# Token operands' remainders one step later on VectorE, and two output accumulators in the statistics' PSUM banks, at the end of layer 1

## The chip, the cores and the metric

The kernel runs on one core of a Trainium2 chip. The metric is the device time of one execution in microseconds (us). Five engines work side by side, each through its own queue in order: TensorE (PE, matrix products into PSUM), VectorE (DVE), ScalarE (ACT), GpSimd (POOL) and SyncE (SP, which issues the DMAs here). They wait for each other through semaphores.

## The reference, cut to what matters

Two layers over 1024 latent tokens of width 1024. Layer 0 mixes by a Fourier transform and differential attention. Layer 1, whose end is the place of the change, is a short gated convolution (`n` is 1024, all in float32):

```python
def short_conv_mixer(proj, conv_w, w_out):
    bg, cg, xt, g = jnp.split(proj, 4, axis=-1)
    u = cg * xt
    ...
    conv = sum(conv_w[t] * up[:, t:t + n] for t in range(CONV_K))
    return (bg * conv * jax.nn.silu(g)) @ w_out
...
    y = short_conv_mixer(h @ odd_w_in[o_i], odd_conv_w[o_i], odd_w_out[o_i])
    ...
    x_lat = x_lat + gate[:, None, :] * y
```

## The kernel before

**Products.** Layer 1 does its two big products (`h @ odd_w_in`, then `y @ odd_w_out`) by a Strassen-like scheme. An output group `g` covers 2 blocks of 128 output features and both halves (512 each) of the tokens. It takes seven products `p` = 1 to 7, written (g, p). Groups 0 to 15 are the input projection, groups 16 to 19 the output projection, 18 and 19 last. Each product combines a weight operand `wop` with four token operands `B[p][k]`, k = 0 to 3. Every operand is split in two, the rounded value and its remainder, so that a product is 4 x 3 matmuls of 128x512 (lines 649 to 651: value by value, value by token remainder, weight remainder by value).

**Accumulators.** The sums of a group stand in three PSUM accumulators: X (products 1, 6, 7, 4 in this order, read out after each), Z (product 2) and Y (products 5, 7 and 3). The pool `acc` has 3 buffers for X, 2 for Y and 1 for Z. The pool `pst`, tag `t`, has 2 more banks; they hold small statistics and transposes earlier in the kernel and nothing at this place. The read-outs of the last four groups are `take` in `finish2` (line 1349, on VectorE): accumulator times gate plus a residual that a DMA has fetched.

**Operands.** `wop` makes a weight operand from raw weights: a rounding copy on ScalarE (line 61), then the remainder on VectorE, or on GpSimd for p = 4 and 7 (line 62). Products 2 and 5 also take additions on GpSimd (line 628). The raw weights of group g + 2 are fetched (`wload`, line 1240) when those of group g are used up. A weight operand is made LEAD = 5 products ahead. `bop` makes a token operand: where the product needs one, a subtraction of two parts of the gated tokens `y` on VectorE (line 1217), then the rounding copy on ScalarE, then the remainder on VectorE, both through `part`.

**Order.** From product (14, 1) on, the order on TensorE, VectorE, ScalarE and GpSimd is that of the code. `order` lists the products:

```python
order += [(16, 1), (16, 5), (17, 1), (17, 5), (16, 2), (16, 6), (17, 2), (17, 6), (16, 7), (17, 7), (16, 4), (16, 3),
          (17, 4), (17, 3)]
```

Before it come (14, 7), (15, 7), (14, 4), (14, 3), (15, 4), (15, 3), behind it the seven of 18 and of 19. `hooks` says behind which product which token operands of the output projection are made: p = 1, 5, 6, 2, 7, 4, 3 between (15, 5) and (17, 1). SP's order is set by a scheduler when the kernel is built.

Of the kernel before, what the change touches and what calls it, by code (L numbers as in the profile page):

```python
# [8 lines left out]
F32 = mybir.dt.float32  # L9
F32R = mybir.dt.float32r  # L10
AF = mybir.ActivationFunctionType
ALU = mybir.AluOpType
# [5 lines left out]
P = 128  # L18
# [11 lines left out]
NB = 512  # L30
# [7 lines left out]
def block_kernel(tc, A):  # L38
    nc = tc.nc
# [3 lines left out]
    def opn(name, side="left", space=None):  # L43
        kw = dict(name=name, bufs=1, side=side, reuse_waits="tile")
        if space is not None:
            kw["space"] = space
        cm = tc.tile_pool(**kw)
        pools[name] = (cm, cm.__enter__())
        return pools[name][1]
# [5 lines left out]
    f32 = lambda t: t.bitcast(F32)  # L55
# [3 lines left out]
    def part(src, o, eng):  # L59

        nc.scalar.copy(out=o[:, 0, :], in_=src)  # L61
        eng.tensor_tensor(out=o[:, 1, :], in0=src, in1=f32(o[:, 0, :]), op=ALU.subtract)  # L62
        return o
# [5 lines left out]
    pst = opn("pst", space=PSUM)  # L69
    acc = opn("acc", space=PSUM)  # L70
# [17 lines left out]
    def load_x(half):  # L88
# [9 lines left out]
        out=cs[:, :, 0:2], in_=small[:, S_C:S_C + 16].rearrange("p (k r) -> p k r", r=2), func=AF.Silu)  # L98
# [5 lines left out]
        out=bias1, in0=small[:, S_B:S_B + 48].rearrange("p (l k) -> p l k", l=2)[:, :, 8:16],  # L104
# [100 lines left out]
    def token_sums(parts, n):  # L205
        ps = pst.tile([P, 8], F32, name="ps_ss", tag="t", bufs=2)
        for i in range(n // P):
            for a in parts:
                nc.tensor.matmul(ps[:, i:i + 1], lhsT=a[:, i * P:(i + 1) * P], rhs=ones[:, 0:1],
                                 start=a is parts[0], stop=a is parts[-1])  # L210
        return ps
# [13 lines left out]
    def ps_rows(dg, n):  # L225

        psr = pst.tile([P, NB], F32, name="ps_r", tag="t", bufs=2)
        nc.tensor.matmul(psr[:, :n], lhsT=ones, rhs=dg[:, :n], start=True, stop=True)
        return psr
# [65 lines left out]
    def proj_tok(tt, c, at=()):  # L295
        ps = acc.tile([P, NB], F32, name="ps_tok", tag="acc", bufs=6)
        for k in range(KT):
            if k in at:
                tick()
            if k == 7:  # L300
                tick(cols)
            proj_step(ps, tt, c, k)
        return ps
# [70 lines left out]
    for k in range(KT):  # L374
        t = hcp.tile([P, TC], F32, name="xc", tag="hc", bufs=17)
# [6 lines left out]
    V, G = nc.vector, nc.gpsimd  # L382
# [66 lines left out]
    ps = token_sums([a0], NB)  # L449
# [148 lines left out]
    for tt in range(NK):  # L598
# [3 lines left out]
        if tt == 0:  # L602
            alds.append(ada_load(*adas[0]))
        ps = proj_tok(tt, 1, (4,))
# [4 lines left out]
                          in_=v.rearrange("p (h d) -> p h d", h=NH))  # L609
# [34 lines left out]
    def quarters(ps, w, x, start, mid=None):  # L644
        for k in range(4):
            if mid and k == mid[0]:
                mid[1]()
            a, b = (w[:, i, k * P:(k + 1) * P] for i in range(2))
            nc.tensor.matmul(ps, lhsT=a, rhs=x[k][0], start=start and k == 0, stop=False, skip_group_check=not start)  # L649
            nc.tensor.matmul(ps, lhsT=a, rhs=x[k][1], start=False, stop=False, skip_group_check=not start)  # L650
            nc.tensor.matmul(ps, lhsT=b, rhs=x[k][0], start=False, stop=k == 3, skip_group_check=not start)  # L651
# [252 lines left out]
    for n, (g, p) in enumerate(order):  # L904
        if ahead:
            q = ahead.pop(0)
# [25 lines left out]
    def w0next(eng=nc.gpsimd):  # L932
        if wq:
            w0half(0, eng)
            w0half(1, eng)
# [139 lines left out]
    def y0(half):  # L1075
        for k in range(KT):
            Y[half][k] = (Yh[half][k], Yl[half][k])

    def proj_feat2(w, half, at={}):
        ps = acc.tile([P, NB], F32, name="ps_feat", tag="acc", bufs=6)  # L1080
        for k in range(KT):
            if k in at:
                at[k]()
            a, b = (w[k // 4][:, i, (k % 4) * P:(k % 4 + 1) * P] for i in range(2))
            nc.tensor.matmul(ps, lhsT=a, rhs=Y[half][k][0], start=k == 0, stop=False)  # L1085
            nc.tensor.matmul(ps, lhsT=a, rhs=Y[half][k][1], start=False, stop=False)  # L1086
            nc.tensor.matmul(ps, lhsT=b, rhs=Y[half][k][0], start=False, stop=k == KT - 1)  # L1087
        return ps
# [63 lines left out]
    acc = opn("acc", space=PSUM)  # L1152
    Y = [[None] * KT for _ in range(2)]
# [36 lines left out]
    def stats1(half):  # L1190
        return rms_diag(token_sums(ssq[half], NB), NB, mp, ("xr", 2))
# [16 lines left out]
        fo_split(*fo, g, nc.gpsimd)  # L1208
    BSRC = {1: 0, 2: 2, 3: 3, 4: 2, 5: 0, 6: 0, 7: 1}

    def bop(p, x, k, eng=None, tt=True):

        q = [*x[k], *x[k + 4 if p not in (1, 5) else k]]
        if tt:
            i = {5: (0, 1, 0), 7: (1, 1, 3), 6: (0, 3, 0), 4: (2, 2, 0)}.get(p)
            if i:
                nc.vector.tensor_tensor(out=q[i[0]], in0=q[i[1]], in1=q[i[2]], op=ALU.subtract)
        o = arena[p - 1][:, k * T:(k + 1) * T].rearrange("p (i t) -> p i t", i=2) if p < 3 else \
            hB.tile([P, 2, NB], F32R, name=f"B{p}", bufs=4)
        B[p][k] = part(q[BSRC[p]], o, eng or nc.vector)  # L1220

    B = {i: [None] * 4 for i in range(1, 8)}

# [7 lines left out]
    def wload(g):  # L1231
        if g < NGR:
            raws[g] = []
            for i in range(2):
                pool = (wp, w2)[g % 2]
                t = pool.tile([P, KT * P], F32, name="wraw", bufs=2)
                if g < 16:
                    nc.sync.dma_start(out=t, in_=A["wodd"][g // 2, ((1, 2), (3, 0))[g % 2][i]])
                else:
                    nc.sync.dma_start(out=t, in_=A["wo1"][2 * (g - 16) + i])  # L1240
                raws[g].append(t)

    def wop(g, p, eng=None):
        pool = wpools[0]
        wpools.append(wpools.pop(0))
        wops[g, p] = wpart(g, p, raws[g], done, lambda: w2.tile([P, NB], F32, name="s1", bufs=1),
                           lambda src, e: part(src, pool.tile([P, 2, NB], F32R, name="wop", bufs=4 if pool is wp else 2), e),
                           eng)
        if p == 3:
            wload(g + 2)  # L1250

    banks = {}

    def product(g, p, mid=None, later=False):
        bank = "ZXZYXYXX"[p]
        start = p in (1, 5, 2)
        if start:
            banks[g, bank] = acc.tile([P, NB], F32, name="ps" + bank, bufs={"X": 3, "Y": 2, "Z": 1}[bank])
        quarters(banks[g, bank], wops.pop((g, p)), [(x[:, 0, :], x[:, 1, :]) for x in B[p]], start, mid)
        fin = finish1 if g < 16 else finish2  # L1260
        if later:
            return lambda: fin(g, p)
        fin(g, p)

    part22 = {}
    us, ysd = {}, []
# [112 lines left out]
    for half in range(2):  # L1379
        y0(half)  # L1380
        for f in range(KT):
            if half == 0 or f < KT - 1:
                w0next()
            if half == 1 and f == KT - 2:
                wload(0)
                wload(1)
            if pend:
                ps = pend.pop(0)
            else:
                ps = proj_feat2(W[half * KT + f], half)  # L1390
            if half == 1 and f == KT - 1:
                for q in order[:5]:
                    wop(*q)
                man.__exit__(None, None, None)
                man = tc.manual_schedule(engines=MANUAL)
                man.__enter__()
            out0(half, f, ps)
            if half == 1 and f == 0:
                dg = stats1(0)
            if half == 1 and f == 1:  # L1400
                r = vv[:, NB:T]
                nc.scalar.copy(out=r, in_=ps_rows(dg, NB))
                mod1(0, range(KT), r)
                for k in range(4):
                    bop(1, x1, k)
                for k in range(4):
                    bop(2, x1, k)

    cls("acc", "pp", "yao")
    acc = opn("wacc", space=PSUM)  # L1410
# [11 lines left out]
    V, G = nc.vector, nc.gpsimd  # L1422
# [77 lines left out]
    for n, (g, p) in enumerate(order):  # L1500
        if n < 12:
            continue
        if (g, p) == (14, 1):
            man.__exit__(None, None, None)
            man = tc.manual_schedule(engines=MANUAL)
            man.__enter__()
        while wn < min(n + LEAD + 1, len(order)):
            wop(*order[wn])
            wn += 1
        product(g, p)  # L1510
        for q, k0, k1 in hooks.get((g, p), ()):
            for k in range(k0, k1):
                bop(q, ysd, k, V)
    man.__exit__(None, None, None)
    cls("hB", "w2", "x1", "m", "w", "wacc", "pst", "at0", "const")

# [100 lines left out]
```

## Time and profile before

| what | value |
|---|---|
| median of 3 runs | 1139.51 us |
| the three runs | 1139.52, 1132.86, 1139.51 us |
| profiled execution, its own time | 1135.15 us |
| its span | 1133.4 us |
| PE busy | 1043.9 us (92% of the span) |
| DVE busy | 763.0 us (67%) |
| mean granted TensorE clock | 0.974 |

The profiled execution is a fourth one beside the three runs. Its span is what the profile covers; 1.75 us of its own time lie around it. Times in views count from the span's start. A timeline row gives the start, the duration, the engine, the line, the operation, what it writes and reads, and in brackets how long the engine was idle before it and who ended that.

### The profile page before, as it was taken

The numbers are of one execution on the slowest core, as the hardware profiler recorded it, in microseconds if no ns is written. First come the engines' busy times: TensorE is split into PE (matmuls) and PEld (weight loads), VectorE is DVE, ScalarE is ACT, GpSimd is POOL, SyncE is SP. The second block draws the span as 40 slices with busy tenths as digits, with TensorE's granted clock in tenths as the row PEclk, the third lists the DMA queues.
The fourth block names the chain that finished last, engine by engine and source line by source line (L and its number), as shares of the span: only waits on it lengthen the run. The fifth ranks groups of instructions, "written<-read, shape, count | busy, mean of one in ns | idle before, by whom it ended". The sixth has DMA issues, their size and how long they took to land.

```text
span 1133.4 us, 14135 instructions
## 1 busy us (share of the span) xinstructions
PE 1043.9 (92%) x5118; PEld 851.1 (75%) x5118; DVE 763.0 (67%) x1073; ACT 480.0 (42%) x868; POOL 498.8 (44%) x422
## 2 busy tenths in 40 slices
PE   4989899989888989999999998889999999998598
PEld 2657688778777878999988876568888888776486
DVE  4599856874868178888873287985645554578642
ACT  4453123311443367777763363633333333343320
POOL 1257103631556236676575455654343444332331
PEclk9999899989899999999999999989999999999799
DMA  9724895434020795271004541121111111111421
GB/s 346 295 94 131 267 296 182 145 112 159 9 93 26 181 262 133 79 182 47 21 20 165 198 165 50 37 75 38 67 46 56 56 57 56 56 67 55 166 76 65
DMA packets 61381, 131.12 MB, mean 116 GB/s; under 512 B 5248, under 2 KB 30208, under 8 KB 58112
## 3 DMA queue, kind: packets, MB, share of 16 engines
q1 hardware_dynamic: 60240, 125.64, 34.8%
q0 software_dynamic: 1072, 4.59, 1.1%
q8 instruction: 40, 0.66, 0.2%
q14 instruction: 29, 0.24, 0.1%
HBM read 105.57 MB, written 24.64 MB: 115 GB/s over the span
## 4 chain that ended last, share of the span: by engine, by line
PE 54%; DVE 16%; POOL 3%; ACT 3%; issue 3%; DMA 3%; SPq 0%; ACTq 0%; DVEq 0%; POOLq 0%
PE psX L649 6%; PE psX L650 6%; PE psX L651 6%; PE ps_av L1032 5%; PE psY L649 3%; PE psY L650 3%; PE psY L651 3%; PE S L982 3%; PE S L983 2%; PE ps_t L1022 2%; DVE nm L987 2%; PE ps_feat L1085 2%; PE ps_feat L1087 2%; PE ps_feat L1086 2%; DVE arena L62 2%
## 5 line engine op out<-in xcount | busy, mean ns | idle before, releaser
L61 ACT CAST wop<-wraw 128x512 fp32r<-128x512 f32 x152 | 93.3, 620 | 130.6 <-PE psY L651 28.0
L62 POOL TENSOR_TENSOR wop<-wraw,wop 128x512 fp32r<-128x512 f32 x72 | 99.7, 1388 | 76.8 <-ACT wop L61 76.4
L284 PE MATMUL ps_tok<-whi,hhi 128*128 128x512 f32 x288 | 119.0, 413 | 3.4 <-ACT hhi L393 2.5
L285 PE MATMUL ps_tok<-whi,hlo 128*128 128x512 f32 x288 | 115.7, 402 | 4.3 <-DVE hlo L397 4.2
L286 PE MATMUL ps_tok<-wlo,hhi 128*128 128x512 f32 x288 | 114.8, 399 | 0.0
L987 DVE TENSOR_REDUCE nm<-S 128x1 f32<-128x1280 f32 x64 | 95.0, 1487 | 22.1 <-PE S L983 20.0
L649 PE MATMUL psX<-B,wop 128*128 128x512 f32 x240 | 97.3, 405 | 9.8 <-ACT c L1293 4.9
L998 ACT ACTIVATE p<-S,nm 128x1280 f32<-128x1280 f32 x64 | 85.2, 1332 | 44.6 <-DVE nm L987 38.9
L650 PE MATMUL psX<-B,wop 128*128 128x512 f32 x240 | 96.9, 404 | 1.5 <-POOL B L1439 1.1
L651 PE MATMUL psX<-B,wop 128*128 128x512 f32 x240 | 96.4, 402 | 0.5 <-POOL wop L62 0.5
L628 POOL TENSOR_TENSOR s<-wraw 128x512 f32<-128x512 f32 x20 | 27.3, 1363 | 120.0 <-DMA wraw<-in_wodd_dram 114.0
L62 DVE TENSOR_TENSOR wop<-wraw,wop 128x512 fp32r<-128x512 f32 x80 | 68.9, 863 | 13.2 <-ACT wop L61 12.9
L628 POOL TENSOR_TENSOR wraw<-wraw 128x512 f32<-128x512 f32 x40 | 56.6, 1421 | 47.9 <-DVE wop L62 40.4
L1032 PE MATMUL ps_av<-v,aT 128*128 128x128 f32 x640 | 76.8, 275 | 0.0
L1032 PEld LDWEIGHTS ps_av<-v,aT 128*128 128x128 f32 x640 | 74.2, 192 | 0.2
L285 PEld LDWEIGHTS ps_tok<-whi,hlo 128*128 128x128 f32 x288 | 55.5, 193 | 18.8 <-DVE hlo L397 8.0
L1009 POOL TENSOR_TENSOR p<-p,cc 128x256 f32<-128x256 f32 x32 | 40.4, 1262 | 65.6 <-DVE cc L1006 46.6
L284 PEld LDWEIGHTS ps_tok<-whi,hhi 128*128 128x128 f32 x288 | 55.7, 193 | 17.8 <-ACT hhi L393 3.7
L649 PE MATMUL psY<-B,wop 128*128 128x512 f32 x160 | 64.1, 400 | 3.6 <-DVE u L1301 1.8
L650 PE MATMUL psY<-B,wop 128*128 128x512 f32 x160 | 64.2, 401 | 0.6 <-POOL B L1439 0.3
L286 PEld LDWEIGHTS ps_tok<-wlo,hhi 128*128 128x128 f32 x288 | 55.4, 192 | 11.9
L651 PE MATMUL psY<-B,wop 128*128 128x512 f32 x160 | 63.7, 398 | 0.0
(344 smaller groups left out, 2671.7 us busy)
## 6 DMA issues: line engine op xcount, KB each, us to landing
ada_raw<-in_ada_dram SPq DMA_DIRECT2D x24, 1024.0 KB, 6.6
wraw<-in_wodd_dram SPq DMA_DIRECT2D x32, 512.0 KB, 3.5
wraw<-in_wo_dram SPq DMA_DIRECT2D x24, 512.0 KB, 3.8
wraw<-in_wtok_dram SPq DMA_DIRECT2D x16, 512.0 KB, 4.2
arena<-kd SPq DMA_DIRECT2D x16, 320.0 KB, 8.6
kq<-kd SPq DMA_DIRECT2D x16, 320.0 KB, 9.7
xt<-in_xT_dram SPq DMA_DIRECT2D x16, 256.0 KB, 5.8
xr<-in_xT_dram SPq DMA_DIRECT2D x16, 256.0 KB, 3.8
```

Source lines behind the costliest of these rows:

```text
L61: nc.scalar.copy(out=o[:, 0, :], in_=src)
L62: eng.tensor_tensor(out=o[:, 1, :], in0=src, in1=f32(o[:, 0, :]), op=ALU.subtract)
L284: nc.tensor.matmul(ps, lhsT=hh, rhs=whi, start=k == 0, stop=False)
L285: nc.tensor.matmul(ps, lhsT=hl, rhs=whi, start=False, stop=False)
L286: nc.tensor.matmul(ps, lhsT=hh, rhs=wlo, start=False, stop=k == KT - 1)
L628: tt = lambda out, x, y, op: nc.gpsimd.tensor_tensor(out=out, in0=x, in1=y, op=op)
L649: nc.tensor.matmul(ps, lhsT=a, rhs=x[k][0], start=start and k == 0, stop=False, skip_group_check=not start)
L650: nc.tensor.matmul(ps, lhsT=a, rhs=x[k][1], start=False, stop=False, skip_group_check=not start)
L651: nc.tensor.matmul(ps, lhsT=b, rhs=x[k][0], start=False, stop=k == 3, skip_group_check=not start)
L987: nc.vector.tensor_reduce(out=nm, in_=S[m][:, :NKEY], op=ALU.max, axis=AX.X, negate=True)
L998: nc.scalar.activation(out=p, in_=S[m][:, :NKEY], func=AF.Exp, bias=tiles.pop((i, m, "nm")), accum_out=z)
L1032: nc.tensor.matmul(ps, lhsT=groups[i, k // 4][:, (k % 4) * P:(k % 4 + 1) * P], rhs=v[:, k * P:(k + 1) * P], start=k == 0, stop=k == NK - 1)
```

## The change

Three things in the code. `bop` no longer calls `part`: the rounding copy is issued on ScalarE as before, and the remainder is put on a list, `lows`. The list is emptied on VectorE by the next `bop`, behind that one's own subtraction (ahead of it where the next `bop` works on the same k, since the subtraction overwrites what the remainder reads), and before a product that needs an operand whose remainder is still on the list. And the accumulators of (16, 5), which is group 16's Y, and of (17, 2), which is group 17's Z, are taken from `pst`, tag `t`, and no more from `acc`.

```diff
-    def bop(p, x, k, eng=None, tt=True):
+    lows = []
+
+    def low():
+
+        for o, src, k in lows:
+            nc.vector.tensor_tensor(out=o[:, 1, :], in0=src, in1=f32(o[:, 0, :]), op=ALU.subtract)
+        lows.clear()
+
+    def bop(p, x, k):
...
+        i = {5: (0, 1, 0), 7: (1, 1, 3), 6: (0, 3, 0), 4: (2, 2, 0)}.get(p)
+        if lows and lows[0][2] == k:
+            low()
+        if i:
+            nc.vector.tensor_tensor(out=q[i[0]], in0=q[i[1]], in1=q[i[2]], op=ALU.subtract)
+        low()
...
-        B[p][k] = part(q[BSRC[p]], o, eng or nc.vector)
+        nc.scalar.copy(out=o[:, 0, :], in_=q[BSRC[p]])
+        lows.append((o, q[BSRC[p]], k))
+        B[p][k] = o
...
-            banks[g, bank] = acc.tile([P, NB], F32, name="ps" + bank, bufs={"X": 3, "Y": 2, "Z": 1}[bank])
+            banks[g, bank] = pst.tile([P, NB], F32, name="ps" + bank, tag="t", bufs=2) if (g, p) in ((16, 5), (17, 2)) \
+                else acc.tile([P, NB], F32, name="ps" + bank, bufs={"X": 3, "Y": 2, "Z": 1}[bank])
...
+        if any(B[p][k] is l[0] for l in lows for k in range(4)):
+            low()
         product(g, p)
```

Line numbers behind the edit move: the token subtraction of line 1217 stands in 1227 afterwards, the token remainder of line 62 in 1216, the read-out of line 1349 in 1363.

**VectorE, at the token operands of p = 5 and 6.** Before, around the products (15, 6) and (15, 2); `B_8194` to `B_8261` are token operands, `y<-y` is a subtraction of line 1217, `wop` the remainder of the weight operand (14, 3), `psZ` a read-out:

```order
L1217 TENSOR_TENSOR y<-y 128x512
L62 TENSOR_TENSOR B_8215<-y,B_8215 128x512 [waits Activation_49]
L1217 TENSOR_TENSOR y<-y 128x512
L62 TENSOR_TENSOR B_8219<-y,B_8219 128x512 [waits Activation_49]
L62 TENSOR_TENSOR wop<-wraw,wop 128x512 [waits Activation_49]
```

The same place afterwards:

```order
L1227 TENSOR_TENSOR y<-y 128x512
L1216 TENSOR_TENSOR B_8194<-y,B_8194 128x512 [waits Activation_49]
L1227 TENSOR_TENSOR y<-y 128x512
L1216 TENSOR_TENSOR B_8215<-y,B_8215 128x512 [waits Activation_49]
L62 TENSOR_TENSOR wop<-wraw,wop 128x512 [waits Activation_49]
L1300 TENSOR_TENSOR y<-y,psZ 128x512 [waits PE_49]
L1227 TENSOR_TENSOR y<-y 128x512
L1216 TENSOR_TENSOR B_8219<-y,B_8219 128x512 [waits DVE_49]
```

Each remainder now stands behind the subtraction of the next operand. The weight remainder kept its place, so one token remainder fewer stands between the last subtraction of a group and it. ScalarE's order is the same before and after.

**TensorE, at the start of (17, 2).** Before, with the last two matmuls of (16, 6) ahead of it:

```order
L650 MATMUL psX<-B_8425,wop 128x512
L651 MATMUL psX<-B_8425,wop 128x512
L649 MATMUL psZ<-arena_2065,wop 128x512 [waits DVE_49,Activation_49]
L650 MATMUL psZ<-arena_2065,wop 128x512
L651 MATMUL psZ<-arena_2065,wop 128x512
```

Afterwards:

```order
L650 MATMUL psX<-B_8425,wop 128x512 [waits DVE_49]
L651 MATMUL psX<-B_8425,wop 128x512
L649 MATMUL psZ<-arena_2065,wop 128x512 [waits Activation_49]
L650 MATMUL psZ<-arena_2065,wop 128x512
L651 MATMUL psZ<-arena_2065,wop 128x512 [waits DVE_49]
```

The first matmul's wait for VectorE (the read-out of group 16's Z) is gone; the third one waits for VectorE's remainder of the weight operand, and the matmul that reads the remainder in `B_8425`, the last token operand of (16, 6), has a wait for it. Nothing else moved on TensorE, and its products keep their order.

**VectorE, at the read-outs of groups 16 and 17.** Before, `B_8502` to `B_8511` are the token operands of p = 3, and `u<-psZ` and `u<-psX` the read-outs of (16, 2) and (16, 6):

```order
L62 TENSOR_TENSOR B_8508<-y,B_8508 128x512 [waits Activation_49]
L62 TENSOR_TENSOR B_8511<-y,B_8511 128x512 [waits Activation_49]
L1349 SCALAR_TENSOR_TENSOR u<-psZ,gate_94,u 128x512 [waits PE_49]
L1349 SCALAR_TENSOR_TENSOR u<-psX,gate_94,u 128x512 [waits DMAHW6_49,PE_49]
L62 TENSOR_TENSOR wop<-wraw,wop 128x512 [waits Activation_49]
```

Afterwards the last of the four, `B_8511`, stands fourteen rows further on, behind the weight remainders of (18, 5) and (18, 6), with the read-out of (16, 4) between them:

```order
L62 TENSOR_TENSOR wop<-s_8647,wop 128x512 [waits Activation_49]
L1363 SCALAR_TENSOR_TENSOR u<-psX,gate_94,u 128x512 [waits PE_49]
L62 TENSOR_TENSOR wop<-wraw,wop 128x512 [waits Activation_49]
L1216 TENSOR_TENSOR B_8511<-y,B_8511 128x512
L1363 SCALAR_TENSOR_TENSOR u<-psY,gate_94,u 128x512 [waits PE_49]
```

The product (16, 3) reads `B_8511` in its last three matmuls. On SP one of the residual fetches (`out<-x1d`, for a late group) moved behind five stores of results and the four weight fetches of groups 18 and 19; the weight fetches and stores keep their order among themselves.

More of the change, by code (lines that the diff above doesn't have):

```diff
@@ L1209, in block_kernel @@
     BSRC = {1: 0, 2: 2, 3: 3, 4: 2, 5: 0, 6: 0, 7: 1}
-    def bop(p, x, k, eng=None, tt=True):
-        q = [*x[k], *x[k + 4 if p not in (1, 5) else k]]
[L1214 to L1217, printed above, removed]
+    lows = []
[4 more added lines that the diff above has]
+    def bop(p, x, k):
+        q = [*x[k], *x[k + 4 if p not in (1, 5) else k]]
+        i = {5: (0, 1, 0), 7: (1, 1, 3), 6: (0, 3, 0), 4: (2, 2, 0)}.get(p)
[4 more added lines that the diff above has]
+        low()
         o = arena[p - 1][:, k * T:(k + 1) * T].rearrange("p (i t) -> p i t", i=2) if p < 3 else \
             hB.tile([P, 2, NB], F32R, name=f"B{p}", bufs=4)
-        B[p][k] = part(q[BSRC[p]], o, eng or nc.vector)
+        nc.scalar.copy(out=o[:, 0, :], in_=q[BSRC[p]])
+        lows.append((o, q[BSRC[p]], k))
+        B[p][k] = o
     B = {i: [None] * 4 for i in range(1, 8)}
@@ L1509, in block_kernel @@
             wn += 1
+        if any(B[p][k] is l[0] for l in lows for k in range(4)):
+            low()
         product(g, p)
@@ L1512, in block_kernel @@
             for k in range(k0, k1):
-                bop(q, ysd, k, V)
+                bop(q, ysd, k)
     man.__exit__(None, None, None)
```

## Prediction

> **What bounds the kernel now.** I read the stages first. The row gives a stretch of the span and, for each engine, its busy time and number of instructions.
>
> ```profile
> 995.00:1015.00 20.00, 19.11 (x81) 14.73 (x79) 15.26 (x18) 9.70 (x18) 8.05 (x6) 1.00 0.22 77
> 1015.00:1042.00 27.00, 23.18 (x84) 17.90 (x84) 23.67 (x38) 9.78 (x18) 7.88 (x6) 0.87 0.18 60
> 1042.00:1066.00 24.00, 9.94 (x39) 7.50 (x40) 19.16 (x29) 10.58 (x19) 7.01 (x5) 0.76 0.29 96
> 1066.00:1130.00 64.00, 62.51 (x263) 49.60 (x261) 26.67 (x36) 9.96 (x16) 17.88 (x14) 0.98 0.28 100
> ```
>
> The columns behind the length are PE, PEld, DVE, ACT, POOL. From 1066 on TensorE works 62.5 of 64 us, so whatever product comes last out of a wait there carries the end with it. From 1042 to 1066 TensorE works 9.9 of 24 us and VectorE 19.2: this is the place where the change can act. Who waits for whom in the span's last 150 us:
>
> ```profile
> PE psZ L649 <- DVE u L1349: 13.2, 1, 13.2
> DVE B L62 <- ACT B L61: 11.0, 16, 0.7
> PE psX L649 <- ACT c L1293: 2.2, 1, 2.2
> PE psY L649 <- DVE u L1301: 1.8, 1, 1.8
> PE psY L649 <- DVE y L1301: 1.4, 1, 1.4
> ```
>
> One wait of TensorE is worth more than all others: 13.2 us, for a read-out of Z. The timeline around it:
>
> ```profile
> 1051.38 0.39 PE L651 MATMUL psX<-B,wop 128*128 128x512 f32 x1
> ...
> 1064.05 0.74 DVE L1349 SCALAR_TENSOR_TENSOR u<-psZ,gate,u 128x512 f32<-128x512 f32 x1
> 1064.71 0.73 DVE L1349 SCALAR_TENSOR_TENSOR u<-psX,gate,u 128x512 f32<-128x512 f32 x1
> ...
> 1064.93 0.77 PE L649 MATMUL psZ<-arena,wop 128*128 128x512 f32 x1 [13.16 <-DVE u L1349]
> ...
> 1069.33 0.39 PE L649 MATMUL psX<-B,wop 128*128 128x512 f32 x1
> ...
> 1072.13 0.39 PE L649 MATMUL psX<-B,wop 128*128 128x512 f32 x1
> ```
>
> At 1051.38 (16, 6) issues its last matmul. (17, 2) needs the only Z buffer, which VectorE reads out at 1064.05, though (16, 2) had filled it before (16, 6) began. TensorE goes on 0.88 us after the read-out's start (1064.93 - 1064.05). (17, 2) then takes 4.40 us, (17, 6) from 1069.33 to 1072.13 only 2.80: that is a product at full rate, 0.233 us a matmul. (16, 7) starts at 1072.13. Its own condition, the read-out of (16, 6) from X at 1064.71, had long been met.
>
> VectorE is late since it does much between products, and since each token operand sends it on a round trip. One of the 16 trips (VectorE's rows, then ScalarE's beside them):
>
> ```profile
> 1007.88 0.68 DVE L1217 TENSOR_TENSOR y<-y 128x512 f32<-128x512 f32 x1
> 1009.25 0.69 DVE L62 TENSOR_TENSOR B<-y,B 128x512 fp32r<-128x512 f32 x1 [0.69 <-ACT B L61]
> 1009.86 0.69 DVE L62 TENSOR_TENSOR wop<-wraw,wop 128x512 fp32r<-128x512 f32 x1
> ...
> 1008.60 0.62 ACT L61 CAST B<-y 128x512 fp32r<-128x512 f32 x1 [1.36 <-DVE y L1217]
> 1009.12 0.62 ACT L61 CAST wop<-wraw 128x512 fp32r<-128x512 f32 x1
> ```
>
> The subtraction starts at 1007.88, ScalarE's copy 0.72 later and ends 0.62 after that; the remainder waits 0.69 us for it. Instructions of VectorE without a wait follow each other every 0.61 us.
>
> **The change, part by part.** *VectorE's order, up to the read-out of (16, 6).* All 16 waits, 11.0 us, leave their place. One token remainder, `B_8511`, moves behind that read-out: another 0.6 us. What comes back stands at the end of each step, where the weight remainder now follows the last subtraction with one token remainder between them. Counted from that subtraction: VectorE is free for it at 2 x 0.61 = 1.22, but ScalarE copies the token operand first and the weight second (0.72 + 0.52 + 0.62 = 1.86, and 0.03 to the start), so it waits 0.67. Five steps are so (weights (14, 3), (15, 3), (17, 1), (17, 2), (17, 6)): 3.35. Before weight (16, 6) nothing stands between: 1.89 - 0.61 = 1.28. Before (16, 1) four copies stand ahead of the weight's, and four remainders beside them: 0.72 + 4 x 0.52 + 0.62 + 0.03 - 5 x 0.61 = 0.4. Two or three first remainders of a step still wait 0.15, since 0.72 + 0.62 + 0.03 is more than 1.22. Together 5.4. Net: -11.0 - 0.6 + 5.4 = -6.2.
>
> GpSimd takes some of that back. The two engines exclude each other:
>
> ```profile
> 1011.06 1.61 DVE L1217 TENSOR_TENSOR y<-y 128x512 f32<-128x512 f32 x1
> ...
> 1010.82 1.30 POOL L62 TENSOR_TENSOR wop<-wraw,wop 128x512 fp32r<-128x512 f32 x1 [4.79 <-ACT wop L61]
> ```
>
> The same subtraction that took 0.68 at 1007.88 takes 1.61 beside a GpSimd instruction, and ends 0.55 after it: a meeting costs 0.93. Where such an instruction fell into one of VectorE's waits, it will now fall on an instruction. There are 17 on GpSimd from 995 to 1066 (6, 6 and 5 in the stages). The bounds are no more meetings (0) and enough of them to eat the whole gain (6 or 7 more). I take 0.4, as most already meet one: VectorE is busy 58.1 of the 71 us. So the read-out of (16, 6) goes from 1064.71 to 1064.71 - 5.8 = **1058.9**.
>
> *The banks.* (17, 2) needs no read-out any more and runs behind (16, 6). (17, 6) needs X of (17, 1):
>
> ```profile
> 1059.90 0.75 DVE L1349 SCALAR_TENSOR_TENSOR out<-psX,gate,out 128x512 f32<-128x512 f32 x1
> ```
>
> 5.8 earlier this is 1054.1, so (17, 6) can start at 1055.0 and ends at 1057.8, or 1059.4 at the slow rate. That is ahead of what (16, 7) waits for: 1058.9 + 0.88 = **1059.8** against 1072.13, -12.3. The earlier waits of 2.2, 1.8 and 1.4 us shorten or go too, and save nothing of their own: they lie ahead of a wait for VectorE, whose order doesn't need those products sooner. The second bank, Y for (16, 5), ends the wait of 1.8 and makes a Y buffer free for (17, 5); both lie ahead of the same wait and get 0.
>
> (17, 7) needs X of (17, 6), two read-outs and a weight remainder further on VectorE: 1058.9 + 0.66 + 1.67 (the row at 1065.37 below) + 0.66 = 1061.9, and 0.88: 1062.8, where TensorE would be at 1062.6. **+0.2**.
>
> *What is late next* is the moved remainder `B_8511`. On VectorE it is queued behind the weight remainders of (18, 5) and (18, 6), and those need raw weights that are fetched only when group 16's are used up:
>
> ```profile
> 1065.37 1.67 DVE L62 TENSOR_TENSOR wop<-wraw,wop 128x512 fp32r<-128x512 f32 x1
> 1067.06 0.81 SPq L1240 DMA_DIRECT2D wraw<-in_wo_dram  x2
> DMA to landing us min/median/max: 3.4/3.7/4.7
> 1072.29 1.30 POOL L628 TENSOR_TENSOR s<-wraw 128x512 f32<-128x512 f32 x1 [0.72 <-DMA wraw<-in_wo_dram]
> 1073.67 1.62 POOL L628 TENSOR_TENSOR wraw<-wraw 128x512 f32<-128x512 f32 x1
> ...
> 1077.41 1.30 POOL L628 TENSOR_TENSOR wraw<-s,wraw 128x512 f32<-128x512 f32 x1 [2.12 <-DVE wop L62]
> ...
> 1080.73 0.75 DVE L1349 SCALAR_TENSOR_TENSOR u<-psX,gate,u 128x512 f32<-128x512 f32 x1 [0.67 <-PE psX L651]
> 1081.44 0.69 DVE L62 TENSOR_TENSOR wop<-wraw,wop 128x512 fp32r<-128x512 f32 x1
> ```
>
> The remainder of (16, 3) ends at 1065.37 + 1.67 = 1067.04, and the fetches go out at 1067.06. Now: 1059.6 + 1.67 = 1061.3. The second goes 0.45 later; with 4.7 it lands at 1066.4 (the GpSimd row at 1072.29, which waits for it, agrees: 5.2 after 1067.06). GpSimd's three additions take 1.30 + 1.62 + 1.30 and 0.1 between: 1070.7. ScalarE's copy 0.62, the remainder of (18, 6) 0.61 and `B_8511` 0.69, with 0.2 of hand-overs: 1072.85. Without a stall (16, 3)'s first matmul on it, its eleventh, would stand at 1062.8 + 2 x 2.80 + 10 x 0.233 = 1070.75. So TensorE waits **+2.1**, between 0 (fetches at 3.4, additions out of VectorE's way) and 4 (a meeting or two more). A pause of that length was followed by the slow rate at (17, 2), at most 4.40 - 2.80 = 1.6; the row that waits 2.2 lies in a stage with a clock of 0.87. I take **+0.5** between 0 and 1.6. Behind it TensorE has no wait of more than 1 us, before as after. The residual fetch that moved on SP serves group 19, tens of microseconds later: 0.
>
> Sum: -12.3 + 0.2 + 2.1 + 0.5 = **-9.5 us**, against the profiled execution's own 1135.15 (span 1133.4 and 1.75 around it): 1125.65, 0.992 of it. The median shown is 1139.51, with one run at 1132.86; the ratio on the median gives 1130.0.
>
> **Rivals.**
>
> *GpSimd eats VectorE's part.* Six or seven more meetings of 0.93 us take the 5.8 back; the banks still act. (16, 7) then starts at 1064.7 + 0.88 = 1065.6, -6.5, and + 0.2 + 2.1: -4.2, 1135.3 on the median. For it: VectorE loses its gaps, where GpSimd got in. Against: it had only 13 us of them. The Trainium skill, "SBUF — State Buffer", section "Who interferes with whom", says that VectorE with two SBUF inputs and GpSimd hold a shared port pair exclusively for the whole instruction, and the row at 1011.06 agrees. It speaks against packing VectorE denser.
>
> *No stall at (16, 3).* The weights land in 3.4 and GpSimd isn't held up: -12.1, 1127.4. For it: the median landing of 3.7. Against: the 5.2 from the first issue in the pair that counts.
>
> *The banks don't help*, as (17, 2) meets another wait (its weight remainder, say): then it starts by the old rule, 5.8 earlier, 1133.7. Against: that remainder stands on VectorE well ahead of the read-out of (17, 1).
>
> *Slower.* The fetch of group 18 holds up (16, 3), two groups ahead of where it is used. Each us that it lands later costs one; with 12.1 us to give, the kernel is slower if it lands more than 4.7 + 10 = 14.7 us after issue, and 2 us beyond that gives 1141.5. For it: the fetches stand on SP in one queue behind stores and residuals that wait for VectorE. Against: no landing above 4.7 in the stage.
>
> **How the numbers follow.** The forecast has 0.62, GpSimd 0.13, no stall 0.17, banks 0.04, slower 0.04. The likeliest gives 1130. The runs shown differ by 0.6%, which I keep at both ends: from the lowest run with the no-stall case (1132.86 - 11.5) to the median with the GpSimd case: 1121.5 to 1135. About 1% is what a measurement can tell here; that is 11.4 us, which needs the no-stall case or a forecast at its good end: faster 0.24, within 1% 0.72, slower 0.04.
>
> **What would show it.** In the profile afterwards: the wait of 13.2 is gone and no wait for `u` from psZ is left; VectorE's 16 waits of 0.69 are replaced by about six for `wop`; the read-out of (16, 6) stands near 1059 and (16, 7) starts 0.9 behind it; TensorE waits some 2 us within (16, 3) for `B`. I am wrong if (16, 7) starts above 1063 (GpSimd), or if (16, 3) has no wait or one of 4 us and more.

## The result, and the profile after

The changed kernel takes 1129.58 us in the median (1127.24 to 1131.34, 7 runs) against 1137.35 of the kernel before (1132.86 to 1139.52, 7 runs): a ratio of **0.9931 [0.9914, 0.9947]**, 7.8 us, within 1%. The forecast was 0.992 and 1130.0 us. The profiled execution of the change took 1128.21 us.

The edit of `bop` also moves the remainders of the input projection's first two token operands, eight instructions on VectorE some 320 us earlier. That is worth nothing: layer 1's first matmul stands 101.03 us behind the same addition of line 1108 on GpSimd before (687.52 and 586.49) and 101.05 after, and 101.04 to 101.07 in the other kernels here. From that matmul to the first of (15, 1) the code is the same, but the time isn't: 301.5 to 304.2 us over all profiles. I therefore count from a common point, the first matmul of (15, 1), which stands ahead of all that changed at the end of the layer. The rows are before's and, in the next fence, after's:

```profile
991.30 0.39 PE L649 MATMUL psX<-arena,wop 128*128 128x512 f32 x1
```

```profile
992.17 0.40 PE L649 MATMUL psX<-arena,wop 128*128 128x512 f32 x1
```

So 0.87 us have to be taken off a time of after to set it beside one of before. Over all profiles here this point lies between 988.8 and 996.0. The last matmul of the program stands 137.76 us behind it before and 129.95 after: **-7.81 us**, the same as the medians give.

The stages afterwards, with the columns of the prediction's table (length, then PE, PEld, DVE, ACT, POOL, granted clock, DMA share, GB/s):

```profile
995.00:1015.00 20.00, 20.00 (x87) 16.09 (x86) 17.64 (x22) 11.71 (x21) 10.10 (x7) 1.00 0.25 79
1015.00:1042.00 27.00, 24.72 (x105) 19.23 (x103) 25.14 (x41) 9.62 (x17) 7.74 (x6) 1.00 0.19 66
1042.00:1066.00 24.00, 18.45 (x60) 13.54 (x61) 21.05 (x29) 10.55 (x19) 7.91 (x5) 0.79 0.37 118
1066.00:1123.00 57.00, 53.15 (x220) 41.72 (x218) 22.73 (x31) 8.70 (x14) 16.06 (x12) 0.97 0.26 99
```

In the stage from 1042 to 1066, where TensorE worked 9.9 us, it now works 18.5. But from 1066 on it is no longer full: 3.9 of 57 us are idle, where 1.5 of 64 were. The waits of the span's last 140 us say where (us in total, times, the longest):

```profile
PE psX L649 <- DVE out L1363: 3.4, 2, 2.4
PE psX L649 <- DVE u L1363: 3.0, 2, 2.5
PE psY L650 <- DVE B L1216: 2.4, 1, 2.4
```

The wait of 13.2 for a read-out of Z is gone. The last line is a new one, for a token operand `B` on a matmul that is not the first of its product. The timeline, VectorE's read-out of (16, 6) first:

```profile
1059.86 0.73 DVE L1363 SCALAR_TENSOR_TENSOR u<-psX,gate,u 128x512 f32<-128x512 f32 x1
...
1055.93 0.47 PE L649 MATMUL psX<-B,wop 128*128 128x512 f32 x1 [2.43 <-DVE out L1363]
...
1060.74 0.48 PE L649 MATMUL psX<-B,wop 128*128 128x512 f32 x1 [0.47 <-DVE u L1363]
...
1074.27 0.76 PE L650 MATMUL psY<-B,wop 128*128 128x512 f32 x1 [2.43 <-DVE B L1216]
1074.82 0.63 PE L651 MATMUL psY<-B,wop 128*128 128x512 f32 x1
1075.25 0.63 PE L649 MATMUL psX<-B,wop 128*128 128x512 f32 x1
...
1077.79 0.39 PE L649 MATMUL psX<-B,wop 128*128 128x512 f32 x1
```

The read-out of (16, 6) is at 1059.86, 1058.99 on before's scale. (17, 6) starts at 1055.93 and (16, 7) at 1060.74, 1059.87 on that scale, where it was 1072.13. At 1074.27 the eleventh matmul of (16, 3) has waited 2.43 us for `B_8511`, and behind it the matmuls stand 0.43 us apart, not 0.23, for eight intervals, to 1077.79. That is the whole account: 12.26 us won at (16, 7), 2.43 lost in the wait, and 3.52 - 8 x 0.233 = 1.66 in the slow matmuls behind it. It comes to -8.2; the remaining 0.4 us are spread over small gaps.

### The profile page after: what moved, and what is told of

It reads as the page before. It is cut to its first block, busy times and chain, and to the rows that moved or that the text cites. A ratio compares the mean times of both kernels' runs of the same rounds, so it can differ in the third digit from the quotient of the medians.

```text
span 1126.4 us, 14132 instructions
## 1 busy us (share of the span) xinstructions
PE 1047.5 (93%) x5118; PEld 854.1 (76%) x5118; DVE 759.8 (67%) x1073; ACT 479.8 (43%) x868; POOL 497.8 (44%) x422
## 4 chain that ended last, share of the span: by engine, by line
PE 56%; DVE 15%; ACT 4%; POOL 4%; issue 3%; DMA 0%; ACTq 0%; DVEq 0%; POOLq 0%
PE psX L649 6%; PE psX L650 6%; PE psX L651 6%; PE ps_av L1032 5%; PE psY L650 3%; PE psY L651 3%; PE psY L649 3%; PE S L982 3%; PE S L983 3%; PE ps_t L1022 2%; DVE nm L987 2%; PE ps_feat L1085 2%; PE ps_feat L1087 2%; PE ps_feat L1086 2%; PE psZ L651 1%
## 5 line engine op out<-in xcount | busy, mean ns | idle before, releaser
L62 DVE TENSOR_TENSOR wop<-wraw,wop 128x512 fp32r<-128x512 f32 x80 | 65.6, 823 | 20.4 <-ACT wop L61 20.1
L649 PEld LDWEIGHTS psX<-B,wop 128*128 128x128 f32 x240 | 46.4, 193 | 26.8 <-issue 5.7
L650 PE MATMUL psY<-B,wop 128*128 128x512 f32 x160 | 63.8, 399 | 2.8 <-DVE B L1216 2.4
L286 PEld LDWEIGHTS ps_tok<-wlo,hhi 128*128 128x128 f32 x288 | 56.6, 197 | 12.3
L651 PE MATMUL psY<-B,wop 128*128 128x512 f32 x160 | 63.5, 397 | 1.5 <-DVE wop L62 1.5
```

The source lines that it names most:

```text
L286: nc.tensor.matmul(ps, lhsT=hh, rhs=wlo, start=False, stop=k == KT - 1)
```

## Experiments

My theory was the prediction's: VectorE's order and the banks each win some 6 us at (16, 7), and the remainder that the change moved takes a part of it back at (16, 3). The rivals were that the new waits on VectorE or GpSimd eat the first part, or that (16, 3) waits for something else.

All times in the table are counted from the first matmul of (15, 1), in us. "Lost" is the wait of more than 0.25 us behind the start of (16, 7), but for the 0.94 us in the last group that every kernel has; the gain is that of the last matmul against 137.76. "No wait" means that (16, 7) follows the product ahead of it without a wait.

| kernel | read-out of (16, 6) | (16, 7) starts | lost | last matmul | gain | ratio of times |
|---|---|---|---|---|---|---|
| before | 73.41 | 80.83 | 0 | 137.76 | | |
| the change | 67.69 | 68.57 | 2.43 | 129.95 | 7.81 | 0.9931 [0.9914, 0.9947] |
| order alone | 67.62 | 75.35, no wait | 0 | 132.31 | 5.45 | 0.9947 [0.9924, 0.9971] |
| banks alone | 73.46 | 74.79, no wait | 0 | 131.97 | 5.79 | 0.9929 [0.9907, 0.9952] |
| bank for Z alone, with the order | 67.66 | 68.54 | 2.47 | 129.98 | 7.78 | 0.9922 [0.9893, 0.9950] |
| moved remainder earlier | 67.69 | 68.58 | 0 | 127.14 | 10.62 | 0.9898 [0.9878, 0.9918] |
| flushed once, after (17, 1) | 69.38 | 70.26 | 0 | 128.76 | 9.00 | 0.9913 [0.9881, 0.9945] |
| flushed after every product | 64.48 | 65.37 | 0 | 122.52 | 15.24 | 0.9834 [0.9819, 0.9848] |
| the same, p = 3 held back | 62.14 | 66.12, no wait | 0 | 123.04 | 14.72 | 0.9850 [0.9816, 0.9884] |

### The order alone

```
-            banks[g, bank] = pst.tile(...) if (g, p) in ((16, 5), (17, 2)) else acc.tile(...)
+            banks[g, bank] = acc.tile([P, NB], F32, name="ps" + bank, bufs={"X": 3, "Y": 2, "Z": 1}[bank])
```

> Only the remainders' order is changed; both accumulators stay in their old pool. Theory (the end hangs on VectorE's read-outs of groups 16 and 17): the read-out of (16, 2) comes 5.7 us earlier than before, (17, 2) still waits for it, for about 7 us instead of 13.2, and runs at the slow rate behind the pause; (16, 3) has no wait, since the remainder of B_8511 now has 6 us more: a gain of 5 to 6 us, ratio 0.995. Rival (the wait in (16, 3) is owed to late weights and comes whatever the banks do): the wait of 2 us in (16, 3) is there too, and the gain is 2 to 3 us.

TensorE still waits for the read-out of Z, a row of its timeline at (17, 2):

```profile
1063.87 0.77 PE L649 MATMUL psZ<-arena,wop 128*128 128x512 f32 x1 [10.96 <-DVE u L1362]
```

The read-out comes 5.8 us earlier than before and the end 5.45 us earlier. There is no wait within (16, 3): TensorE reaches it later, when `B_8511` has its remainder. So the gain is the theory's, and the rival, with the stall already here, fell. The wait itself is 10.96 us and not the 7 expected: TensorE ends (16, 6) 3.6 us earlier too, which the estimate had left out.

### The banks alone

```
+            banks[g, bank] = pst.tile([P, NB], F32, name="ps" + bank, tag="t", bufs=2) if (g, p) in ((16, 5), (17, 2)) \
+                else acc.tile([P, NB], F32, name="ps" + bank, bufs={"X": 3, "Y": 2, "Z": 1}[bank])
```

> Only the two accumulators move; the remainders stand where they stood before. Theory: VectorE keeps its 16 waits of 0.69, the read-out of (16, 6) stays at 1064.7, and (16, 7) starts 0.9 behind it instead of at 1072.1: a gain of 6 to 6.5 us, ratio 0.995, and no wait in (16, 3). Rival (the wait of 13.2 us is worth its length once the bank is there): a gain of 11 to 13 us, ratio 0.990.

```profile
1056.30 0.50 PE L649 MATMUL psZ<-arena,wop 128*128 128x512 f32 x1 [2.60 <-ACT wop L61]
...
1061.86 0.74 DVE L1350 SCALAR_TENSOR_TENSOR out<-psX,gate,out 128x512 f32<-128x512 f32 x1
...
1062.75 0.77 PE L649 MATMUL psX<-B,wop 128*128 128x512 f32 x1 [3.04 <-ACT B L61]
```

(17, 2), the first row, no longer waits for a read-out, but for its own weight operand. (17, 6) at 1062.75 waits 3.04 us. The profile names the copy of a token operand, but (16, 6) had already used all token operands of (17, 6). What (17, 6) needs is the X bank of (17, 1), whose read-out on VectorE's unchanged order, the middle row, starts at 1061.86; the product follows 0.89 us behind it, as it does in the change (1055.93 behind 1055.04). Behind the pause it runs at the slow rate and takes 5.26 us, so (16, 7) starts at 1068.01, 0.45 us later than the read-out of (16, 6) at 1066.68 would let it. The end is 5.79 us earlier: just short of the theory's 6 to 6.5, and not by the theory's condition, since (16, 7) has no wait left. The rival, 11 to 13, fell.

The two parts together should give 5.45 + 5.79 = 11.24 us; the change gives 7.81. At (16, 7) they do add up, and a little more: it starts 5.48 and 6.04 us earlier in the two kernels, 12.26 in the change. What is missing is a loss behind it that neither part has by itself: the wait of 2.43 in (16, 3) and the 1.66 of slow matmuls behind that. It needs both, the moved remainder from the order and an early (16, 3) from the banks.

### One bank instead of two

```
-            ... if (g, p) in ((16, 5), (17, 2)) \
+            ... if (g, p) in ((17, 2),) \
```

> The change with only (17, 2)'s Z in the statistics' banks; (16, 5)'s Y is back in its old pool. Theory (only the read-outs of groups 16 and 17 set the end): (16, 5) and (17, 5) wait for Y again, some 1 to 3 us each, ahead of the place that counts, and the time is that of the change: 7 to 8.5 us below the kernel before in the profile, ratio 0.993. Rival (each wait of TensorE counts): 1.5 to 3 us slower than the change, ratio 0.995 to 0.996.

```profile
1030.67 0.47 PE L649 MATMUL psY<-B,wop 128*128 128x512 f32 x1 [1.33 <-DVE u L1315]
1039.48 0.77 PE L649 MATMUL psY<-B,wop 128*128 128x512 f32 x1 [2.98 <-DVE y L1315]
```

(16, 5) waits 1.33 us and (17, 5) 2.98 us again, and the end is the same to 0.03 us. The second bank is worth nothing, as predicted: its waits lie ahead of a later one for VectorE, and VectorE doesn't need those products sooner.

### The moved remainder ahead of the next weights

This kernel empties the list ahead of the weight operands that are prepared at (16, 3), and so puts `B_8511` ahead of the remainder of (18, 6). Nothing else moves.

```
+        if (g, p) == (16, 3):
+            low()
         while wn < min(n + LEAD + 1, len(order)):
```

> The change, with the remainder of B_8511 ahead of the weight remainder of (18, 6) instead of behind it. Theory (it waits for group 18's weights through the queue): the wait in (16, 3) shrinks from 2.4 us to 0.5 to 1.5, since (18, 5) still stands ahead, and all before it stays: 8.5 to 10.5 us below the kernel before, more where the slow rate goes with the shorter wait. Rival (it waits for the read-out of (16, 4) alone): the wait stays above 2 us and the time that of the change, 7.9 us.

VectorE's rows at that place, TensorE's first and ninth matmul of the slow stretch at (16, 7), and the eleventh matmul of (16, 3):

```profile
1072.58 1.12 DVE L1216 TENSOR_TENSOR B<-y,B 128x512 fp32r<-128x512 f32 x1
1073.85 0.69 DVE L62 TENSOR_TENSOR wop<-wraw,wop 128x512 fp32r<-128x512 f32 x1
...
1061.52 0.60 PE L649 MATMUL psX<-B,wop 128*128 128x512 f32 x1 [1.80 <-DVE u L1363]
...
1064.89 0.50 PE L651 MATMUL psX<-B,wop 128*128 128x512 f32 x1
...
1073.88 0.40 PE L650 MATMUL psY<-B,wop 128*128 128x512 f32 x1
```

The read-out of (16, 6) and the start of (16, 7) are where the change has them, the wait in (16, 3) is gone, and the end comes 2.8 us sooner. Two things made the wait go. `B_8511` ends 1.3 us earlier (80.76 us behind (15, 1), 82.05 in the change), as it no longer stands behind the weight remainder of (18, 6), which in the change waits 1.16 us for its copy. And TensorE comes later, since this execution met the slow matmuls at (16, 7): 1061.52 to 1064.89 is 3.37 us for eight intervals, 1.5 more than at 0.233. So the matmul at 1073.88 finds the remainder that ended at 1073.70. Without the slow matmuls it would have stood at about 1072.4 and waited some 1.3 us, an estimate from these rows. The 0.5 to 1.5 that I had expected to remain are thus not refuted, only hidden, and that no wait shows is luck. The rival, that (16, 3) waits for the read-out of (16, 4) alone, gave no such 1.3 us, and fell. In the next two kernels `B_8511` stands ahead of all of group 18's weights and ends over 10 us before its product needs it; there the wait is gone without such help. What held (16, 3) up is so shown: the place of `B_8511` behind the weights of group 18.

### Emptying the list after every product

```
         for q, k0, k1 in hooks.get((g, p), ()):
             for k in range(k0, k1):
                 bop(q, ysd, k)
+        low()
```

> The change, and the list of remainders is emptied at the end of each step's hooks, ahead of the next weight remainder. Theory (new waits at the step ends, and the late B_8511): the waits for the weight copies shrink from about 5 us to 1 or 2, the read-out of (16, 6) comes another 2 to 3 us earlier than with the change, (16, 3) has no wait and no slow rate: 13 to 15 us below the kernel before, ratio 0.987 to 0.989. Rival (GpSimd takes whatever VectorE saves): the read-out stays where the change has it, and only the wait and the slow rate at (16, 3) go: 11 to 12 us, ratio 0.990.

VectorE's waits for copies of ScalarE between 990 and 1066 in the kernel before (first fence) and in the change (second), and in the same stretch, counted from (15, 1), of this kernel (third):

```profile
DVE B L62 <- ACT B L61: 11.0, 16, 0.7
DVE wop L62 <- ACT wop L61: 1.5, 1, 1.5
```

```profile
DVE wop L62 <- ACT wop L61: 5.9, 8, 1.5
```

```profile
DVE wop L62 <- ACT wop L61: 2.7, 2, 1.5
DVE B L1216 <- ACT B L1231: 1.4, 2, 0.7
```

The wait of 1.5 stands in all three. The change turned 16 waits for token operands (11.0 us) into seven for weights (5.9 - 1.5 = 4.4 us). Emptying the list at the step's end leaves two for token operands (1.4) ahead of the read-out of (16, 6); its other one for a weight, 1.2, lies behind it. It also puts `B_8511` ahead of group 18's weights as well. Four remainders in a row, ahead of the read-outs of group 16, in the change and, with the read-outs of (17, 1) and (16, 6) beside them, here:

```profile
1055.70 3.58 DVE L1216 TENSOR_TENSOR B<-y,B 128x512 fp32r<-128x512 f32 x4
```

```profile
1049.58 0.74 DVE L1363 SCALAR_TENSOR_TENSOR out<-psX,gate,out 128x512 f32<-128x512 f32 x1
1050.24 2.49 DVE L1216 TENSOR_TENSOR B<-y,B 128x512 fp32r<-128x512 f32 x4
...
1053.31 0.74 DVE L1363 SCALAR_TENSOR_TENSOR u<-psX,gate,u 128x512 f32<-128x512 f32 x1
...
1050.47 0.47 PE L649 MATMUL psX<-B,wop 128*128 128x512 f32 x1 [0.88 <-ACT B L1231]
1054.20 0.47 PE L649 MATMUL psX<-B,wop 128*128 128x512 f32 x1 [0.69 <-ACT wop L61]
```

Here the four escape a GpSimd instruction that the change meets: 1.1 us. The read-out of (16, 6) comes another 3.2 us earlier, TensorE's waits at (17, 6) and (16, 7) come to 0.88 and 0.69 us, (16, 3) has none, and the end is 15.24 us ahead of before. The two waits are put down to ScalarE, but they are still for VectorE's read-outs: (17, 6) starts at 1050.47, 0.89 behind that of (17, 1), and (16, 7) at 1054.20, 0.89 behind that of (16, 6), the distance that it has in the other kernels. The theory said 13 to 15; the rival, in which GpSimd takes the gain, fell. This kernel has the lowest median here: 1118.32 us (1117.45 to 1119.84, 4 runs) against 1136.91. The medians differ by 18.6, over 3 more than the last matmul's place explains; 2.5 of them in the profiled pair lie ahead of (15, 1). They are no gain of this edit, since the change, with the same code up to there, reaches that point 3.3 us later in its profile. Why that part is shorter here wasn't tried.

### Emptying it once

```
+        if (g, p) == (17, 1):
+            low()
```

> The change, with the list emptied once, behind the hooks of (17, 1), so that B_8511 stands with the other three of its product as before. Theory: the read-out of (16, 6) comes 0.6 us later than with the change, the wait of 2.43 us and the slow rate of some 1.6 us at (16, 3) go: 10 to 11.5 us below the kernel before in the profile, ratio 0.990. Rival (the pause in (16, 3) comes from late weights or late read-outs whatever the place): 7 to 8 us, as with the change.

```profile
1054.07 5.27 DVE L1216 TENSOR_TENSOR B<-y,B 128x512 fp32r<-128x512 f32 x5
...
1060.81 0.77 PE L649 MATMUL psX<-B,wop 128*128 128x512 f32 x1 [2.13 <-DVE u L1363]
```

This moves `B_8511` back to where it stood before the change. The wait in (16, 3) goes with the slow matmuls behind it, and (16, 7) pays: the read-out comes not 0.6 but 1.7 us later, and the slow matmuls come here, behind the wait of 2.13 (the product takes 4.37 us for 2.80). The fence shows why: five remainders in 5.27 us, where four took 3.58. One is 0.6, and the other 1.1 are one more meeting with the four GpSimd instructions that run there in a row. The net gain over the change is 1.2 us in the trace, in the times not separable from it (0.9913 [0.9881, 0.9945]). The direction was right, the size a microsecond short.

### Taking the four remainders of p = 3 out of the way

On top of the emptying after every product, the remainders of p = 3 wait until the read-outs of group 16 are issued:

```
-        if lows and lows[0][2] == k:
+        if p != 3 and lows and lows[0][2] == k:
...
-        low()
+        if p != 3:
+            low()
...
+        if (g, p) not in ((17, 1), (17, 5), (16, 2), (16, 6), (17, 2), (17, 6)):
+            low()
```

> The list emptied at the end of each step, but the four remainders of p = 3 moved behind the read-outs of (17, 1), (16, 2), (16, 6), (17, 2), (17, 6) and (16, 7). Theory: these read-outs come 2.4 us earlier than with the list emptied at each step, but TensorE itself is by then the bound at (17, 6): only 0.5 to 1.5 us are left to gain, ratio 0.982 to 0.983 to the kernel before. Rival (VectorE's read-outs still bound): 2 to 2.5 us below the kernel with the list emptied at each step, ratio 0.981.

```profile
1053.00 0.74 DVE L1364 SCALAR_TENSOR_TENSOR out<-psX,gate,out 128x512 f32<-128x512 f32 x1
...
1053.89 0.47 PE L649 MATMUL psX<-B,wop 128*128 128x512 f32 x1 [2.14 <-DVE out L1364]
```

The read-out of (16, 6) comes 2.3 us earlier than with the emptying alone, and the end doesn't: 14.72 us against 15.24, in the times not separable. The rows show why. (17, 6) waits for the read-out of (17, 1), at 1053.00, and that one never stood behind the remainders of p = 3: it is 60.82 behind (15, 1), with the emptying alone 60.75. So (17, 6) starts at 61.71 for 61.64. Behind its wait it runs at the slow rate here and takes 4.41 us, and (16, 7) follows without a wait. At full rate (16, 7) would have started at 61.71 + 2.80 = 64.51, 0.86 ahead of the emptying alone, an estimate from these rows and within my 0.5 to 1.5; the slow matmuls took it, so that this gain isn't shown. The rival, 2 to 2.5 us more, fell. The read-outs of group 16 no longer set the end here; the read-out of (17, 1) still does.

## Why the prediction was right, and where not

**VectorE up to the read-out of (16, 6).** Predicted 1058.9, measured 1058.99 on before's scale. The total hides two errors that cancel. The new waits are 4.4 us in seven pieces, not 5.4. Two of the weight remainders, with the wait in brackets:

```profile
1008.38 0.69 DVE L62 TENSOR_TENSOR wop<-wraw,wop 128x512 fp32r<-128x512 f32 x1 [0.60 <-ACT wop L61]
...
1043.88 0.69 DVE L62 TENSOR_TENSOR wop<-wraw,wop 128x512 fp32r<-128x512 f32 x1 [1.20 <-ACT wop L61]
```

Five are of 0.60 (0.67 worked out), one of 1.20 (1.28), one of 0.19 (0.4); the 0.15 at a step's first remainder, of which the sum had two or three, don't show. Against that GpSimd cost 1.2, not 0.4. VectorE's busy time from its first arena remainder to the read-out, before and after:

```profile
995.96:1064.71 68.75, 50.20 (x197) 38.48 (x195) 56.79 (x82) 29.09 (x52) 20.73 (x15) 0.88 0.22 75
```

```profile
996.83:1059.86 63.03, 55.67 (x221) 43.26 (x219) 57.35 (x80) 29.60 (x53) 21.33 (x15) 0.93 0.24 80
```

It rose by 0.56 with one remainder (0.6) fewer in it: 1.2 us, about one meeting more than before, where I had taken less than half a one. With these, -11.0 - 0.6 + 4.4 + 1.2 = -6.0, and the 0.3 to the measured -5.7 are small gaps. The Trainium skill, "SBUF — State Buffer", section "Who interferes with whom", whose exclusive port pair I had set against the change, isn't contradicted (three token remainders that meet a GpSimd instruction take 1.78 or 1.79 us instead of 0.68), but it takes 1.2 of the 11.0 us that the waits gave.

**The banks.** (17, 6) was to start at 1055.0 and starts at 1055.06 on before's scale; (16, 7) at 1059.8 and starts at 1059.87: -12.26 for -12.3. The wait ahead of (17, 7), +0.2, came to less than 0.1. The bank for (16, 5) at 0 is shown by the kernel without it.

**The moved remainder.** This chain, from the fetch on SP to `B_8511`, came out link by link:

```profile
1062.24 0.81 SPq L1253 DMA_DIRECT2D wraw<-in_wo_dram  x2
...
1067.88 1.30 POOL L628 TENSOR_TENSOR s<-wraw 128x512 f32<-128x512 f32 x1 [4.51 <-DMA wraw<-in_wo_dram]
...
1070.62 1.61 POOL L628 TENSOR_TENSOR wraw<-s,wraw 128x512 f32<-128x512 f32 x1
...
1072.27 0.62 ACT L61 CAST wop<-wraw 128x512 fp32r<-128x512 f32 x1 [2.43 <-POOL wraw L628]
...
1072.92 0.69 DVE L62 TENSOR_TENSOR wop<-wraw,wop 128x512 fp32r<-128x512 f32 x1 [1.16 <-ACT wop L61]
1073.53 0.69 DVE L1216 TENSOR_TENSOR B<-y,B 128x512 fp32r<-128x512 f32 x1
```

Less 0.87, the fetch goes out at 1061.37 (1061.3 predicted), the first addition starts at 1067.0 (1066.4), the last ends at 1071.4 (1070.7), `B_8511` ends at 1073.35 (1072.85). The wait is 2.43 for 2.1. The difference is a landing 0.6 later than I took; one of the three additions met VectorE (1.61 instead of 1.30), as in the sum.

**The step that was off** is the slow rate behind that wait, "+0.5 between 0 and 1.6". It was 1.66, at the upper bound. The prediction calls the pause at (17, 2) one "of that length", but that pause was 13.16 us. The kernel before had two pauses of about the length in question:

```profile
1016.36 0.50 PE L649 MATMUL psX<-B,wop 128*128 128x512 f32 x1 [2.19 <-ACT c L1293]
1033.97 0.61 PE L649 MATMUL psY<-B,wop 128*128 128x512 f32 x1 [1.80 <-DVE u L1301]
```

The products behind them took 4.45 and 4.41 us instead of 2.80, which is 1.6 each. I had settled between nothing and 1.6 instead of taking these rows. With 1.6 the sum would have been -8.4 against the -7.81 measured.

**Luck in the number.** That the forecast of 1130.0 us meets the measured 1129.58 is partly luck. The sum was -9.5 us, 1.7 too much: 1.2 in the slow rate, 0.3 in the wait, the rest mostly small gaps that it didn't have. And its ratio was put on a median of 1139.51 us, which over seven runs is 1137.35, 2.2 less. The lower end of the range also uses 11.5 us for the case without a stall, where the sum gives 12.1.

**The rivals.** GpSimd eating VectorE's part, banks that don't help, and a late landing that makes it slower are all refuted by the rows above. No stall at (16, 3) is refuted too, but the kernel with `B_8511` moved shows what it would have been worth: 10.6 us, not the 12.1 I gave it, since that profile has the slow matmuls at (16, 7) instead.

## What to carry to other kernels

A step that defers the last piece of its work must say where that piece goes when no next step comes at once: here one line that empties the list at each product's end doubled the gain (15.2 us for 7.8), as the leftover neither blocks nor is blocked. Two changes that each win 5.5 us don't add up if the second brings TensorE early to something that the first made late; look for the instruction that was moved, and read what stands ahead of it in its engine's queue and what that waits for. And when an engine that isn't the bound loses its waits, count how many of its instructions will meet one of an engine that it excludes, rather than taking a share. Where the profile's releaser of a wait can't be the one, compare distances: each X product here that waits for a read-out on VectorE starts 0.88 to 0.90 us behind the start of the read-out of its bank, whatever engine is named.

## What was not expected of the hardware

TensorE's slow stretch behind a pause has neither a fixed place nor one length. Behind the wait of 2.43 us at 1074.27 it begins at once and ends at 1077.79, 3.5 us later. Behind another of 2.43 us, at 1055.93, the first five matmuls run at full rate. And at (16, 6) in the same profile, behind a wait of 2.52, it lasts 5.2 us, twelve intervals:

```profile
1045.38 0.77 PE L649 MATMUL psX<-B,wop 128*128 128x512 f32 x1 [2.52 <-DVE u L1363]
...
1050.56 0.39 PE L649 MATMUL psZ<-arena,wop 128*128 128x512 f32 x1
```

In the kernel with the order alone, behind a wait of 2.97, this is how it begins and ends:

```profile
1043.97 0.59 PE L651 MATMUL psY<-B,wop 128*128 128x512 f32 x1
1044.36 0.63 PE L649 MATMUL psY<-B,wop 128*128 128x512 f32 x1
...
1047.34 0.43 PE L650 MATMUL psZ<-arena,wop 128*128 128x512 f32 x1
```

It lasts 3.4 us, from 1.2 us behind the restart on. The four stretches here that begin some way behind a restart and run to their end without another wait all last 3.36 to 3.38 us. Those that begin with the restart last from 3.0 us to 6.1 (fourteen intervals, in the kernel that empties the list after every product). And in the kernel with the remainder moved, the wait of 2.29 at (17, 6) is followed by twelve matmuls at full rate, and the slow ones come behind the next wait, at (16, 7). Eight intervals of 0.43 instead of 0.233 cost 1.5 to 1.7 us, fourteen about 2.8, unless another wait falls into them and hides a part.

The Trainium skill, "TensorE: Matmul & The Clock Gate", "Part 1: The HAM clock gate", has the clock decided in free-running windows of 3.413 us, and 426.7 ns between cold matmuls of 512 columns. The spacing, the wandering start and the 3.4 us of the stretches that begin late agree with that. It also has the clock fall after an idle window of about 3.4 us; here pauses of 1.8 to 3 us were enough. The length of the pause alone doesn't decide it: behind 2.19 us at 1016.36 the kernel before ran slow, behind 2.17 us at the same product the kernel with the banks alone did not.
